# Half of an MLP's down projection by seven half-size products in five chunks of eight

## The chip, the cores and the metric

One NeuronCore of one Trainium2 chip runs the whole program. The metric is the device time in microseconds of one execution; the figure before is the median of three runs. One more execution was taken with the profiler, and all rows quoted here come from it.

## The reference, cut to what matters

Two layers over 512 tokens of width 1024. Each layer ends with a squared-ReLU MLP of hidden width 4096, added to the scaled residual and normalised:

```python
def sq_relu_mlp(h, w_up, w_down):
    return jnp.square(jax.nn.relu(h @ w_up)) @ w_down

for layer in range(DEPTH):          # DEPTH = 2
    mix = mixer_a(...) if layer < N_A else mixer_b(...)
    h = layer_norm(DN_ALPHA * h + mix, ln_g[layer, 0], ln_b[layer, 0])
    h = layer_norm(DN_ALPHA * h + sq_relu_mlp(h, mlp_w_up[layer], mlp_w_down[layer]),
                   ln_g[layer, 1], ln_b[layer, 1])
```

Everything is float32. The kernel splits each operand of a large product into a high part `hi` (rounded to the matmul's fp32r format) and a low part `lo = x - hi`, and adds three matmuls: hi by hi, hi by lo, lo by hi.

## The kernel before, in words

**The MLP's chunks.** `mlp` cuts the hidden width into eight chunks (`c`) of 512 features. A pass of the chunk loop does two halves (`n` = 0, 1). A half has an *up phase*, which makes 256 features of the **next** chunk's hidden tile (a `Pair` of feature blocks), and then a *down phase*, which multiplies the present chunk's hidden tile by the columns `n*512` to `n*512+511` of the down weights and adds the result to `res`.

**The up phase.** A `Pair` does its 1024 x 256 by 512 product by a Winograd form of Strassen's scheme: seven products `m1`, `m6`, `m2`, `m7`, `m5`, `m4`, `m3`, in this order, each of 12 matmuls with 256 moving columns. Its weight sums `sa` and `sb` are four instructions on GpSimd (lines 1058 to 1061), each of 128x512. `split0`, `split_b`, `split_a` and `split2` make the hi parts on ScalarE (a cast, line 975) and the lo parts on VectorE (a subtraction, line 976). VectorE reads the partial sums out of PSUM in between: `u2` (line 1107) after `m6`, `u3` (line 1117) after `m7`, and the `r` pieces (lines 1122, 1126, 1130). As `m6`, `m7` and `m4` accumulate in one PSUM tile, `m7` waits for `u2`'s read, `m4` for `u3`'s, and `m3` for the first `r` read.

**The down phase.** For each of four token tiles, `down` issues 12 matmuls of 512 moving columns (4 contraction blocks times three), and VectorE adds the PSUM tile to `res` (line 1149). The weights come as two slabs of 128x1024 (`dn_slab`, `wload`: a DMA at line 105, a cast at line 108 on ScalarE, a subtraction at line 109 on VectorE).

**Between the phases.** While the down phase runs, the weights of the next pair arrive (line 1056), GpSimd makes its four sums, and `split0`, `split_b`, `split_a` prepare it. `close` squares the hidden pieces and splits them (`hh` on ScalarE, `hl` on VectorE, line 983).

**What sets the order.** Each engine runs its instructions in a fixed order. A planner sets it when the program is built, from the order of the source and the readiness that it expects; `behind(a, b)` forces `a` behind `b` on one engine. Raw weights pass through four slots of 4 KB per partition (tag `wr`), hi and lo parts through five each (`wh`, `wl`). All the weight DMAs are issued by SyncE's queue, in order. The small `pad` tiles shift the addresses of the tiles behind them. Chunk 7's down projection is `downs_last`, with the layer norm between its tiles.

Of the kernel before, what the change touches and what calls it, by code (L numbers as in the profile page):

```python
# [11 lines left out]
F32 = mybir.dt.float32  # L12
# [38 lines left out]
def trunk(ctx: ExitStack, tc: tile.TileContext, xT, xn, memT, wk, wq, wv, wqm, wz, wmk, wmv, wo0, wo1, up, dn,  # L51
# [31 lines left out]
    def nm(s):  # L83
        uid[0] += 1
        return f"{s}_{uid[0]}"
# [3 lines left out]

    def mmt(n="mm"):  # L90
        return pmm.tile([P, 512], F32, tag="mm", name=nm(n))

# [3 lines left out]
    def fr(ap):  # L96
        return ap.bitcast(F32)
# [762 lines left out]

    def load_gb(i):
        g_t = late[0].tile([P, D], F32, tag="lng", name=nm("lng"), bufs=1)
        b_t = late[0].tile([P, D], F32, tag="lnb", name=nm("lnb"), bufs=1)
# [61 lines left out]
    lnp = late[0]  # L925
    gb0 = load_gb(0)
    cosT = lnp.tile([P, NT, 32], F32, tag="cosT", name="cosT")
# [32 lines left out]

    def mlp(pool, layer, last, gb0):
        NC = 8
# [4 lines left out]
        def f4(shape, n):  # L967
            return pool.tile(shape, F32, tag="f4", name=nm(n), bufs=5)

# [16 lines left out]
        def new_hid():  # L986
            return hid_tiles(F32R)
# [23 lines left out]
        def ups_second(hid):  # L1011

            for f in range(2):
                w = wload(up[layer, 4 + f], [P, KT, P])
                ps = mmt("up")
                feature_major(ps, w, x_all(XH), x_all(XL))
                r = f4([P, 512], "relu")
# [8 lines left out]
        def x_sums():  # L1026
# [3 lines left out]
            if layer == 0:  # L1030
                f11, f12, f21, f22 = (xf[j][:, :, t] for j in range(2) for t in (tA, tB))
            else:
                f11, f12, f21, f22 = t1, *(f4([P, 4, HT], n) for n in ("f12", "f21", "f22"))
                for f, x in ((f11, x11), (f12, x12), (f22, x22), (f21, x21)):
                    V.tensor_tensor(f, fr(x[0]), fr(x[1]), op=ALU.add)
# [17 lines left out]
        def up_load(f, e):  # L1053
            raw = [wpool[0].tile([P, KT, P], F32, tag="wr", name=nm("wr"), bufs=wpool[1]) for _ in range(2)]
            for i in range(2):
                SY.dma_start(raw[i], up[layer, f + i])
            sa, sb = (f4([P, 2, 4, P], n) for n in ("sa", "sb"))
            e.tensor_tensor(sa[:, 0], raw[1][:, kA], raw[1][:, kB], op=ALU.add)  # L1058
            e.tensor_tensor(sb[:, 0], sa[:, 0], raw[0][:, kA], op=ALU.subtract)  # L1059
            e.tensor_tensor(sa[:, 1], raw[0][:, kA], raw[1][:, kA], op=ALU.subtract)  # L1060
            e.tensor_tensor(sb[:, 1], raw[0][:, kB], sb[:, 0], op=ALU.subtract)
            return raw, sa, sb

# [8 lines left out]
        class Pair:  # L1072


            def __init__(self, f0, e=G):
                self.f0 = f0
                self.raw, self.sa, self.sb = up_load(f0, e)

            def split0(self, first):
                hi, lo = split(self.raw[0], [P, KT, P], first=first)  # L1080
                self.A11, self.A12 = (hi[:, kA], lo[:, kA]), (hi[:, kB], lo[:, kB])

            def split_b(self):
                hi, lo = split(self.sb, [P, 2, 4, P])
                self.S2, self.S4 = ((hi[:, i], lo[:, i]) for i in range(2))

            def split_a(self, first=None):
                hi, lo = split(self.sa, [P, 2, 4, P], first=first)
                self.S1, self.S3 = ((hi[:, i], lo[:, i]) for i in range(2))

            def split2(self, first_act=None):
                self.A22 = split(self.raw[1][:, kB], [P, 4, P], "w2h", first_act=first_act)

# [15 lines left out]
            def m2(self):  # L1109
                product(self.a, self.A12, xq["B21"], False, True)  # L1110
                self.r = f4([P, 2, 512], "r")
                A.activation(self.r[:, 0, tA], self.a, AF.Relu)

# [10 lines left out]
            def m4(self):  # L1124
                product(self.b, self.A22, xq["T4"], False, True)
                V.tensor_tensor(self.r[:, 1, tA], self.s1, self.b, op=ALU.add)

# [23 lines left out]
        def dn_slab(c, n, i, *first):  # L1151
            return wload(dn[layer, c, n, i], [P, 2, 512], *first)

        def dn_slabs(c, n):
            return [dn_slab(c, n, i) for i in range(2)]

        def downs_last(hid):
            c = NC - 1
# [25 lines left out]
            ln_out(*late_out)  # L1184

        hid, nxt = ups_first()
        gb1 = done = None
        tables = rotary_tables(pool) if layer == 0 else None
        for c in range(NC - 1):
            later = new_hid()  # L1190
            for n in range(2):
                p, nxt = nxt, None
                f0 = 4 * c + 2 * n + 6
                early = c == n == 0
                if p is None:
                    ups_second(later)
                    slabs = dn_slabs(c, n)
                else:
# [18 lines left out]
                    done = p.last  # L1217
                if layer == 0 and c == 0:
                    ln_gain(gb0, ALPHA, n)
# [6 lines left out]
                if f0 < 4 * NC:  # L1226
                    nxt = Pair(f0)
                down(c, 0, n, hid, slabs)
                if nxt:
                    nxt.split0(p and p.r22)  # L1230
                down(c, 1, n, hid, slabs)
                if nxt:
                    nxt.split_b()
                down(c, 2, n, hid, slabs)
                if nxt:
                    nxt.split_a()
                down(c, 3, n, hid, slabs)
            if c == 1:
                gb1 = load_gb(2 * layer + 1)
            hid = later  # L1240
        downs_last(hid)

    with tc.tile_pool(name="mlp0", bufs=2) as mpl:
        mlp(mpl, 0, False, gb0)
    hid_pool[0].close()


    with tc.tile_pool(name="l1", bufs=2) as lp:
# [166 lines left out]

        gb0 = load_gb(2)
        run_steps(LAYER1_ORDER, {"w": load_slabs, "k": shared_kv, "q": projq, "a": attend, "F": flush, "o": out1,
# [3 lines left out]
    with tc.tile_pool(name="mlp1", bufs=2) as mpl:  # L1421
        mlp(mpl, 1, True, gb0)
    hid_pool[0].close()
# [70 lines left out]
```

## Time and profile before

| what | value |
|---|---|
| median of 3 runs | 1158.35 us (1158.11 to 1158.95) |
| profiled execution, its own time | 1156.52 us |
| its span | 1154.8 us |
| granted TensorE clock, mean | 0.994 |
| busy: TensorE matmul / VectorE / ScalarE / GpSimd | 1135.5 / 820.1 / 560.0 / 240.3 us |
| weights loaded for the two MLPs | 64 DMAs of 512 KB each for `up` and for `dn` |

The span is the profiled part of that execution; its own time is 1.7 us more. "Busy" is the union of an engine's instructions; a weight load (PEld) overlaps the matmuls. Since matmuls are pipelined, a matmul's recorded 276 or 390 ns is longer than its pace, which is read from the chain of work (pieces with a start, a length and a count). A row of a group gives the line, engine, operation, output and inputs with shapes, the count, the busy time and the mean of one in ns, then the idle time before and what ended it. Rows of the timeline give start and duration in us.

### The profile page before, as it was taken

Reading aid. Unit: us, or ns where it says so; the run is one execution under the profiler, and the core shown is the slowest. Engines: PE = TensorE matmul, PEld = TensorE weight load, DVE = VectorE, ACT = ScalarE, POOL = GpSimd, SP = SyncE. Lnnn points to the kernel's source line nnn. Section 1 sums busy time; section 2 is a strip of 40 time slices with the busy share of each in tenths; the row PEclk is TensorE's granted clock in tenths of the full one; section 3 lists DMA queues with packets and bytes.
Section 4 is the critical chain, followed back from the end, with each engine's and each line's share of the span. In section 5 each row is a group of like instructions: output and inputs, shape, how many; then the busy total and the mean of one; then the engine's idle time right before and its main releaser. Section 6 shows DMA issues by size and latency. Waiting matters only on the chain.

```text
span 1154.8 us, 19153 instructions
## 1 busy us (share of the span) xinstructions
PE 1135.5 (98%) x7578; PEld 1006.6 (87%) x7578; DVE 820.1 (71%) x1562; ACT 560.0 (48%) x1015; POOL 240.3 (21%) x172
## 2 busy tenths in 40 slices
PE   9999999999999999999999999999999999999997
PEld 9878789989998898998988887778988998989986
DVE  6667789767887676666665968886976665666657
ACT  6454843465584444454443336652645444444531
POOL 1112120011022242423320100000042432424203
PEclk9999999899999999999999999999999999999999
DMA  8522132304313243322334231102332332323311
GB/s 298 162 75 78 47 94 66 102 19 172 103 56 128 92 130 108 109 93 91 117 103 127 77 108 55 56 20 74 110 128 92 104 116 91 110 93 110 108 56 73
DMA packets 41258, 114.11 MB, mean 99 GB/s; under 512 B 11536, under 2 KB 12304, under 8 KB 41168
## 3 DMA queue, kind: packets, MB, share of 16 engines
q1 hardware_dynamic: 40736, 112.10, 29.9%
q8 instruction: 59, 0.97, 0.3%
q10 hardware_dynamic: 432, 0.79, 0.2%
q14 instruction: 31, 0.25, 0.1%
HBM read 109.46 MB, written 3.41 MB: 98 GB/s over the span
## 4 chain that ended last, share of the span: by engine, by line
PE 87%; DVE 6%; issue 2%; ACT 2%; POOL 1%; DMA 0%; DVEq 0%; ACTq 0%; POOLq 0%; SPq 0%
PE dn L69 30%; PE upb L69 9%; PE upd L69 6%; PE upa L69 6%; PE wo L69 5%; PE up L69 4%; PE kq L69 4%; PE projqMM L69 3%; PE proj_zMM L69 3%; PE v L69 3%; PE ov L69 1%; PE ssc L69 1%; DVE wl L109 1%; PE VM L69 1%; PE spt L72 1%
## 5 line engine op out<-in xcount | busy, mean ns | idle before, releaser
L108 ACT CAST wh<-wr 128x1024 fp32r<-128x1024 f32 (+1 forms) x124 | 130.5, 1053 | 218.8 <-PE dn L69 154.8
L109 DVE TENSOR_TENSOR wl<-wr,wh 128x1024 fp32r<-128x1024 f32 (+1 forms) x124 | 168.4, 1359 | 69.7 <-ACT wh L108 69.3
L69 PE MATMUL dn<-wh,hh 128*128 128x512 f32 (+1 forms) x516 | 200.2, 388 | 0.0
L69 PE MATMUL dn<-wh,hl 128*128 128x512 f32 (+1 forms) x516 | 200.1, 388 | 0.0
L69 PE MATMUL dn<-wl,hh 128*128 128x512 f32 (+1 forms) x516 | 200.1, 388 | 0.0
L1149 DVE TENSOR_TENSOR res<-res,dn 128x512 f32<-128x512 f32 (+1 forms) x121 | 82.1, 678 | 64.4 <-PE dn L69 64.3
L69 PEld LDWEIGHTS dn<-wh,hl 128*128 128x128 f32 x516 | 96.9, 188 | 19.9
L69 PEld LDWEIGHTS dn<-wh,hh 128*128 128x128 f32 x516 | 96.9, 188 | 18.9
L69 PEld LDWEIGHTS dn<-wl,hh 128*128 128x128 f32 x516 | 96.9, 188 | 18.9
L1058 POOL TENSOR_TENSOR sa<-wr 128x512 f32<-128x512 f32 x26 | 37.1, 1427 | 358.3 <-DMA wr<-in_up_dram 358.3
L825 POOL TENSOR_TENSOR rs<-rs,nhalf 128x1 f32<-128x1 f32 x16 | 13.0, 815 | 307.4 <-DVE rs L824 253.6
L69 PE MATMUL upb<-TH,wh 128*128 128x256 f32 x216 | 60.3, 279 | 0.0
L69 PE MATMUL upd<-XL,wh 128*128 128x256 f32 x216 | 59.8, 277 | 0.5 <-DVE XL L1204 0.5
L69 PE MATMUL upd<-XH,wh 128*128 128x256 f32 x216 | 59.8, 277 | 0.2 <-DVE r L1122 0.2
L69 PE MATMUL upa<-XL,wh 128*128 128x256 f32 x216 | 59.9, 277 | 0.0
L69 PE MATMUL upd<-XH,wl 128*128 128x256 f32 x216 | 59.7, 276 | 0.0
L69 PE MATMUL upa<-XH,wl 128*128 128x256 f32 x216 | 59.7, 276 | 0.0
L69 PE MATMUL upb<-TL,wh 128*128 128x256 f32 x216 | 59.7, 276 | 0.0
L69 PE MATMUL upb<-TH,wl 128*128 128x256 f32 x216 | 59.7, 276 | 0.0
L1060 POOL TENSOR_TENSOR sa<-wr,wr 128x512 f32<-128x512 f32 x26 | 59.1, 2272 | 0.0
L1059 POOL TENSOR_TENSOR sb<-sa,wr 128x512 f32<-128x512 f32 x26 | 54.7, 2104 | 0.0
L975 ACT CAST wh<-wr 128x1024 fp32r<-128x1024 f32 x27 | 28.5, 1054 | 53.6 <-PE upa L69 53.6
(414 smaller groups left out, 3253.5 us busy)
## 6 DMA issues: line engine op xcount, KB each, us to landing
wr<-in_up_dram SPq DMA_DIRECT2D x64, 512.0 KB, 3.7
wr<-in_dn_dram SPq DMA_DIRECT2D x64, 512.0 KB, 3.8
wr<-in_wo_dram SPq DMA_DIRECT2D x16, 512.0 KB, 4.1
wr<-in_bw_dram SPq DMA_DIRECT2D x8, 512.0 KB, 4.2
wr<-in_wk_dram SPq DMA_DIRECT2D x6, 512.0 KB, 4.3
wr<-in_wq_dram SPq DMA_DIRECT2D x6, 512.0 KB, 3.5
wr<-in_wv_dram SPq DMA_DIRECT2D x6, 512.0 KB, 3.5
wr<-in_wz_dram SPq DMA_DIRECT2D x4, 520.0 KB, 3.9
```

Source lines behind the costliest of these rows:

```text
L69: return self.note(nc.tensor.matmul(*args, **kw))
L72: return self.note(nc.tensor.transpose(*args, **kw))
L108: behind(A.copy(hi, raw), first_act)
L109: behind(V.tensor_sub(lo, raw, fr(hi)), first)
L825: G.tensor_tensor(rs, rs, nhalf[:, 0:1], op=ALU.pow)
L975: behind(A.copy(hi, raw), first_act)
L1058: e.tensor_tensor(sa[:, 0], raw[1][:, kA], raw[1][:, kB], op=ALU.add)
L1059: e.tensor_tensor(sb[:, 0], sa[:, 0], raw[0][:, kA], op=ALU.subtract)
L1060: e.tensor_tensor(sa[:, 1], raw[0][:, kA], raw[1][:, kA], op=ALU.subtract)
L1149: V.tensor_tensor(dst, dst, ps, op=ALU.add)
```

## The change

In chunks 2 to 6 (`SD`) of both layers, the down projection's columns 512 to 1023 are computed by the seven-product scheme (`Down`: the hidden tile is the left factor, cut by contraction blocks and by token halves; the weights are the right one, cut by contraction blocks and by 256 columns). Columns 0 to 511 stay as plain products, as two `Quarter`s of 256 columns each, one in each half. All the down matmuls of these chunks have 256 moving columns. The sums of the hidden tile (`Sums`, four GpSimd instructions of 128x512) and those of the weights (four more in `Down`) are new, and so are the splits of the sums. Partial results stay in PSUM and are accumulated further while VectorE adds each state to the place of `res` that it belongs to. Down weights are loaded as four tiles of 256 columns (two DMAs of 256 KB each). Splits get forced places behind named reads. Tags for PSUM tiles become one per bank; `f4` goes from five buffers to three with new tags `r` (three) and `tb` (one). The layer norm's gain and shift rows move to other tiles and are loaded at other places, and the reserved scratch of SBUF shrinks.

```diff
+    def mmt(n="mm", bank=None):
+        if bank is None:
+            bank = turn_of[0] % 3
+            turn_of[0] += 1
+        return pmm.tile([P, 512], F32, tag=f"mm{bank}", name=nm(n), bufs=1)
...
-            return pool.tile(shape, F32, tag="f4", name=nm(n), bufs=5)
+            return pool.tile(shape, F32, tag="f4", name=nm(n), bufs=3)
+        def rt(shape, n):
+            return pool.tile(shape, F32, tag="r", name=nm(n), bufs=3)
+        def tb(n):
+            return pool.tile([P, 4, 256], F32, tag="tb", name=nm(n), bufs=1)
...
+        SD = range(2, NC - 1)
+        nA, nB = slice(512, 768), slice(768, 1024)
+        class Quarter:
+            def __init__(self, c, m):
+                self.c, self.m = c, m
+                self.raw = columns(c, 0, m)
+            def split(self, *first):
+                self.w = split(self.raw, [P, 4, 256], "wh", *first)
+            def tile(self, t, hid):
+                (hh, hl), (wh, wl) = hid, self.w
+                ps = smt("dnq")[:, 0:256]
+                for k in range(4):
+                    h, l = (x[:, k, t * P:(t + 1) * P] for x in hid)
+                    T.matmul(ps, h, wh[:, k, :], start=k == 0, stop=False)
+                    T.matmul(ps, h, wl[:, k, :], start=False, stop=False)
+                    T.matmul(ps, l, wh[:, k, :], start=False, stop=k == 3)
+                dst = res[:, t, self.m * 256:self.m * 256 + 256]
+                return V.tensor_tensor(dst, dst, ps, op=ALU.add)
+        def columns(c, n, m):
+            raw = wpool[0].tile([P, 4, 256], F32, tag="wr", name=nm("wr"), bufs=wpool[1])
+            for i in range(2):
+                SY.dma_start(raw[:, 2 * i:2 * i + 2, :], dn[layer, c, n, i][:, :, m * 256:m * 256 + 256])
+            return raw
+        class Down:
+            def __init__(self, c):
+                self.R0, self.R1 = (columns(c, 1, m) for m in range(2))
+                self.tb = tb("tb")
+            def sums(self, first):
+                b11, b21, b12, b22 = (r[:, i:i + 2, :] for r in (self.R0, self.R1) for i in (0, 2))
+                t3 = self.tb[:, 0:2, :]
+                behind(G.tensor_tensor(t3, b22, b12, op=ALU.subtract), first)
+                G.tensor_tensor(b12, b12, b11, op=ALU.subtract)
+            def sums_2(self):
+                t1, b22 = self.R1[:, 0:2, :], self.R1[:, 2:4, :]
+                G.tensor_tensor(self.R0[:, 0:2, :], b22, t1, op=ALU.subtract)
+            def sums_3(self, first):
+                behind(G.tensor_tensor(self.tb[:, 2:4, :], self.R0[:, 2:4, :], self.R0[:, 0:2, :], op=ALU.subtract),
+                       first)
...
+            def product(self, ps, h, f, t, w, start, stop, rows, cols):
+                (hh, hl), (wh, wl) = h, w
+                for j in range(2):
+                    tk = slice(t.start + j * P, t.start + j * P + P)
+                    for k in range(2):
+                        a, b = (x[:, f + k, tk] for x in h)
+                        T.matmul(ps[:, j, :], a, wh[:, k, :], start=start and j == 0 and k == 0, stop=False,
+                                 skip_group_check=True)
+                        T.matmul(ps[:, j, :], a, wl[:, k, :], start=False, stop=False, skip_group_check=True)
+                        T.matmul(ps[:, j, :], b, wh[:, k, :], start=False, stop=stop and k == 1, skip_group_check=True)
+                for rw, cl in zip(rows, cols):
+                    dst = res[:, rw.start // P:rw.stop // P, cl]
+                    self.out = V.tensor_tensor(dst, dst, ps, op=ALU.add)
...
+        class Sums:
+            def __init__(self, r0, r1):
+                self.r = r0, r1
+                a11, a21, a12, a22 = (r[:, :, t] for r in self.r for t in (tA, tB))
+                G.tensor_tensor(a22, a21, a22, op=ALU.add)
+                G.tensor_tensor(a21, a11, a21, op=ALU.subtract)
+                G.tensor_tensor(a11, a22, a11, op=ALU.subtract)
+                self.last = G.tensor_tensor(a12, a12, a11, op=ALU.subtract)
...
+                if fast and n == 0:
+                    q = Quarter(c, 0)
+                    d = Down(c)
+                    d.hid = hid
+                    d.sums(s_.last)
...
                     p.m6()
-                    p.split2(None if early else done)
-                    slabs = [dn_slab(c, n, 0, p.u2_in, p.m1_out)] if early else dn_slabs(c, n)
+                    p.split2(None if early else done, p.u2_in if fast else None)
+                    if not fast:
+                        slabs = [dn_slab(c, n, 0, p.u2_in, p.m1_out)] if early else dn_slabs(c, n)
+                    elif n == 0:
+                        q.split(p.u2_in, p.m1_out)
+                    else:
+                        d.split_1(p.u2_in, p.m1_out)
                     p.m2()
                     p.m7()
...
+                    if fast and n == 0:
+                        d.split_0(p.u3_in, p.m2_out)
+                        d.sums_2()
+                    if fast and n == 1:
+                        q.split(p.u3_in, p.m2_out)
                     p.m5()
+                    if fast and n == 0:
+                        d.split_t2(p.r22, p.m2_out)
+                        d.s = [s_.split(0, p.r22, p.m2_out)]
+                    if fast and n == 1:
+                        d.s.append(s_.split(1, p.r22, p.m2_out))
                     p.m4()
+                    if fast and n == 1:
+                        d.split_2(p.r21, p.m2_out)
                     p.m3()
...
                 if f0 < 4 * NC:
                     nxt = Pair(f0)
...
+                if n == 1 and c + 1 in SD:
+                    sums = Sums(rs_[0], rs_[1])
...
+                elif n == 0:
+                    d.sums_3(nxt.sums)
+                    q.tile(0, hid)
+                    d.m1()
+                    nxt.split0(d.out, p.last)
+                    q.tile(1, hid)
+                    d.m2()
+                    nxt.split_b(d.out, p.last)
+                    o = q.tile(2, hid)
+                    d.m6()
+                    nxt.split_a(o, p.last)
+                    q.tile(3, hid)
+                    q = Quarter(c, 1)
+                else:
+                    d.m5()
+                    if nxt:
+                        nxt.split0(d.out, p.last)
+                    q.tile(0, hid)
+                    d.m7()
+                    o = q.tile(1, hid)
+                    if nxt:
+                        nxt.split_b(o, p.last)
+                    d.m3()
+                    if nxt:
+                        nxt.split_a(d.out, p.last)
+                    q.tile(2, hid)
+                    q.tile(3, hid)
+                    d.m4()
-            if c == 1:
-                gb1 = load_gb(2 * layer + 1)
+            s_ = sums
+            if c == NC - 2:
+                gb1 = load_gb(2 * layer + 1, *(f4([P, D], n) for n in ("lng", "lnb")))
             hid = later
...
-    nc = bacc.Bacc("TRN2", target_bir_lowering=False, num_devices=1)
+    nc = bacc.Bacc("TRN2", target_bir_lowering=False, num_devices=1, dynamic_dma_scratch_size=256)
```

More of the change, by code (lines that the diff above doesn't have):

```diff
@@ L959, in rotary_tables, with mlp @@
         yield
-    def mlp(pool, layer, last, gb0):
+    def mlp(pool, layer, last):
         NC = 8
@@ new lines, in mlp, with split @@
+        class Sums:
[6 more added lines that the diff above has]
+                self.last = G.tensor_tensor(a12, a12, a11, op=ALU.subtract)
+            def split(self, i, first, first_act):
+                hi, lo = (pool.tile([P, 2, 512], F32R, tag=f"S{n}{i}", name=nm(f"S{n}{i}"), bufs=1) for n in "HL")
+                behind(A.copy(hi, self.r[i]), first_act)
+                behind(V.tensor_sub(lo, self.r[i], fr(hi)), first)
+                return hi, lo
@@ L1184, in downs_last @@
             ln_out(*late_out)
+        pool.tile([P, 16], F32, tag="pad5", name=nm("pad5"), bufs=1)
+        gbt = [pool.tile([P, 2, 512], F32, tag=f"S{n}0", name=nm("gb"), bufs=1).rearrange("p a b -> p (a b)")
+               for n in "HL"]
+        for n in "HL":
+            pool.tile([P, 2, 512], F32, tag=f"S{n}1", name=nm("gb"), bufs=1)
+        pool.tile([P, 48], F32, tag="pad6", name=nm("pad6"), bufs=1)
+        if layer == 0:
+            gb0 = load_gb(0, *gbt)
         hid, nxt = ups_first()
@@ L1188, in mlp @@
         tables = rotary_tables(pool) if layer == 0 else None
+        sums = None
+        rs_ = {}
         for c in range(NC - 1):
             later = new_hid()
+            fast = c in SD
             for n in range(2):
```

97 lines of the change are left out of this document (62 added, 35 removed).

## The prediction

> **What bounds the kernel now.** I read the page first (busy shares, the chain that ended last), then the chain through one half of a chunk, then the busy times of one chunk.
>
> ```profile
> PE 1135.5 (98%) x7578; PEld 1006.6 (87%) x7578; DVE 820.1 (71%) x1562; ACT 560.0 (48%) x1015; POOL 240.3 (21%) x172
> ...
> PE 87%; DVE 6%; issue 2%; ACT 2%; POOL 1%; DMA 0%; DVEq 0%; ACTq 0%; POOLq 0%; SPq 0%
> ...
> 423.23 1.38 PE upa L69 x12
> 424.60 1.36 PE upb L69 x12
> 425.96 1.36 PE upa L69 x12
> ...
> 431.40 1.36 PE upd L69 x12
> 432.76 10.89 PE dn L69 x48
> ...
> 930.10:971.07 40.97, 40.97 (x266) 37.19 (x265) 25.69 (x33) 18.58 (x23) 14.24 (x8) 1.00 0.32 103
> ...
> 654.81 5.65 PE ropeMM L69 x48
> ```
>
> The chain lies 87% on TensorE. A half of a chunk is seven up products (one of 1.38, six of 1.36, so 9.54 us) and 48 down matmuls (10.89 us), with no gap: 20.43 us, or 40.87 us per chunk. In the chunk at 930 us VectorE was busy for 25.7 of 41 us, ScalarE for 18.6 and GpSimd for 14.2. So TensorE bounds the MLPs, at the full granted clock (1.00), and a down matmul saved is time saved as long as no other resource fills up.
>
> **TensorE, per changed chunk.** Removed: 96 matmuls of 512 columns at 10.89/48 = 226.9 ns, 21.78 us. Added: 96 of 256 columns for the quarters and 7 x 12 = 84 for the products, 180 in all. A 256-column matmul takes 1.36/12 = 113.3 ns in the up products, which share the MLP's slots with the new ones, and 5.65/48 = 117.7 ns in `ropeMM`, whose stationary side is token slices as in the new ones. By the first, 20.40 us; by the second, 21.19. I take the first: today's down matmuls pace at twice 113.4 with the same hidden tiles. Saved: 1.38 us (0.59 at least), which makes a chunk 39.49 us (40.28) if TensorE still bounds it. Ten chunks change (five in each layer).
>
> The Trainium skill (TensorE: Matmul & The Clock Gate, Back-to-back issue gap) gives the gap of a warm matmul as N/2.4 plus 2.5 ns, so two halves cost more than a whole. By that formula the saving would be 1.06 us per chunk; the rows here show 113.3 against 226.9 ns, no surcharge, and I keep them.
>
> **What the other engines get.**
>
> ```profile
> L1149 DVE TENSOR_TENSOR res<-res,dn 128x512 f32<-128x512 f32 x8 | 5.5, 682 | 4.8 <-PE dn L69 4.8
> ...
> L1117 DVE TENSOR_TENSOR u<-m,upb 128x256 f32<-128x256 f32 x2 | 0.8, 422 | 3.5 <-PE upb L69 3.5
> ...
> L108 ACT CAST wh<-wr 128x1024 fp32r<-128x1024 f32 x4 | 4.2, 1054 | 10.9 <-PE dn L69 10.9
> ...
> 413.06 1.22 DVE L976 TENSOR_TENSOR wl<-wr,wh 128x1024 fp32r<-128x1024 f32 x1
> 414.19 1.22 DVE L976 TENSOR_TENSOR wl<-sb,wh 128x1024 fp32r<-128x1024 f32 x1
> ...
> 478.94 0.68 DVE L976 TENSOR_TENSOR w2l<-wr,w2h 128x512 fp32r<-128x512 f32 x1
> 479.54 0.68 DVE L1149 TENSOR_TENSOR res<-res,dn 128x512 f32<-128x512 f32 x1
> ```
>
> ScalarE: four slab casts become seven of 128x1024 and a half one (two quarters, `R0`, `R1`, `tb`, two of `Sums`; `T2`): 3.5 x 1.05 = 3.7 us more, 18.6 + 3.7 = 22.3 of 39.5 us. Hidden by the matmuls.
>
> VectorE: the same 3.5 subtractions more at a pitch of 1.13 us (413.06 to 414.19), and eight adds of 682 ns become eight of 256 columns (422) and seven of 512: 25.7 + 4.0 + 2.7 = 32.4 of 39.5 us, if nothing makes it wait.
>
> GpSimd: eight sums per chunk become sixteen.
>
> **The shared path.** This is where I expect the gain to go. Four sums and two slab subtractions in today's chunk:
>
> ```profile
> 483.38 1.31 POOL L1058 TENSOR_TENSOR sa<-wr 128x512 f32<-128x512 f32 x1 [13.43 <-DMA wr<-in_up_dram]
> 484.65 2.30 POOL L1060 TENSOR_TENSOR sa<-wr,wr 128x512 f32<-128x512 f32 x1
> 486.91 2.27 POOL L1059 TENSOR_TENSOR sb<-sa,wr 128x512 f32<-128x512 f32 x1
> 489.26 1.31 POOL L1061 TENSOR_TENSOR sb<-wr,sb 128x512 f32<-128x512 f32 x1
> ...
> 484.29 1.48 DVE L109 TENSOR_TENSOR wl<-wr,wh 128x1024 fp32r<-128x1024 f32 x1 [1.76 <-ACT wh L108]
> 485.70 0.68 DVE L1149 TENSOR_TENSOR res<-res,dn 128x512 f32<-128x512 f32 x1
> 486.30 1.74 DVE L109 TENSOR_TENSOR wl<-wr,wh 128x1024 fp32r<-128x1024 f32 x1
> 487.96 0.41 DVE L1107 TENSOR_TENSOR u<-m,upb 128x256 f32<-128x256 f32 x1
> ```
>
> Alone a sum takes 1.31 us and a subtraction 1.22. Together they take turns: the subtraction issued at 486.30 ends at 488.04, 1.09 us after the sum before it ended (486.95); the sum issued at 486.91 ends at 489.18, 1.14 us after that subtraction. Adds that read PSUM are not delayed (0.68 at 485.70). So GpSimd's sums and VectorE's instructions with two SBUF inputs must fit one after the other into a chunk.
>
> The Trainium skill (SBUF — State Buffer, SBUF: two separate sides) says the same in stronger words: the pair of ports that the two engines share is an exclusive lock held for a whole instruction, against a VectorE operation with two SBUF inputs or in a two-port mode. By that rule the holds add up, as they do here; if the ports shared their bandwidth instead, there would be no such sum and the chunk would be TensorE's 39.49 us, the first rival.
>
> Holds in a changed chunk: VectorE has 15 subtractions of 1.13 (six for pairs, two `hl`, two quarters, `R0`, `R1`, `tb`, two sums) and three half ones of 0.60 (two `w2l`, `T2`; 478.94 to 479.54): 18.75 us. GpSimd has 16 sums of 1.14 (queued) to 1.31 (alone); I take 1.20, since most will be queued: 19.2. Together 37.95 us of 39.49, 96%; today it is 12 x 1.13 + 2 x 0.60 + 8 x 1.20 = 24.4 of 40.87, 60%.
>
> That leaves 1.5 us of idle path, and one hole is longer.
>
> ```profile
> wr<-in_up_dram SPq DMA_DIRECT2D x64, 512.0 KB, 3.7
> wr<-in_dn_dram SPq DMA_DIRECT2D x64, 512.0 KB, 3.8
> ...
> GB/s 234 266 8 0 16 0 52 242 214 0 0 0 60 301 171 250 226 8 0 0 270 234 4 16 0 0 75 309 123 0 0 0 32 298 179 218 270 20 0 0
> ...
> 472.77 0.33 SPq L1056 DMA_DIRECT2D wr<-in_up_dram  x1
> ...
> lng<-in_lng_dram SPq DMA_DIRECT2D x4, 512.0 KB, 4.1
> ```
>
> By four slots in turn, the second half's pair takes the slot of `R1`, which `split_1` frees: `m6` ends 2.74 us into the half, `u2` 0.33 later, `w2l` 0.60, the subtraction 1.13, so at 4.8; SyncE's issue takes 0.33, landing 3.7, and the second 512 KB some 1.75 more at the 300 GB/s that the row's best slices show. GpSimd can start at 10.6. It should have ended the first half's pair sums so that `split_b` (1.05 cast, 1.13 subtraction) is ready for `m6` at 1.38, and does `sums_3` behind them: it falls idle at about 0.4. In these 10.2 us VectorE holds the path for `split_b`, `split_a`, `w2l`, `R1`, the quarter, `s[1]` and `tb`, 6 x 1.13 + 0.60 = 7.4. Idle: 2.8 us.
>
> Elsewhere the queues meet badly. In the first half's up phase GpSimd still has the sums of the hidden tile and of `Down`, so every subtraction can wait 1.20 for the path, and behind it in VectorE's queue stand `u2`, `u3` and the first `r` read, each due within one product (1.36 us) or TensorE stops. The worst is 1.20 + 1.13 + 0.33 - 1.36 = 1.3 us each, 3.9 in all; the least is 0. With half of them met, at half the price, 1.0: an estimate.
>
> Chunk: 37.95 + 2.8 + 1.0 = 41.75 us, 0.88 above today's 40.87 (ends: 39.49, if the idle is overlapped, and 43.5, with sums at 1.31). Ten chunks: +8.8.
>
> **Edits together at nothing.** The tags, slots and scratch: no DMA here is written by GpSimd. The same down bytes come in eight DMAs of 256 KB instead of four of 512, 4 x 0.33 us more of SyncE's issue; rows of 1 KB may land later than 3.8 us, at worst twice that, 7.6. Cover: a quarter is issued behind `sums_3`, about 9 us before its first tile; with 7.6 and 2.2 for its split it would be 1 us late. Gain and shift rows (4.1 us each) now load in chunk 6, whose second half fetches no pair; they delay four slabs whose first use is 10 us later. None of this lies on the chain: 0, ends -1 and +2.
>
> **The sum.** The profiled execution's own time is 1156.52 us, 1154.8 span and 1.7 around it; with +8.8 it is 1165.3. The median shown lies 1.83 above that execution, so 1167.1.
>
> **The rivals.**
> *The path has room and TensorE stays the bound* (the other side). It decides where holds and idle come below 40.87: with 3.8 us idle, at (40.87 - 18.75 - 3.8)/16 = 1.145 us per sum, and the row above shows 1.14 for one queued sum, so it is near. For it: the forced places put each subtraction right behind a read, which spares the reads, and the sums may be issued earlier than four slots in turn allow. Against: 96%. Down to 39.49 it gives 1158.35 - 13.8 = 1144.5; at 117.7 ns 1152.5. Chance 0.36.
> *The two cancel*: 40.87 again, 1158.35. Chance 0.10.
> *GpSimd's chain is late as well.* In one period `split_1`, the load, four pair sums, four of `Sums`, `sums`, `sums_2`, four pair sums, `split_b` and `m6` follow each other: fifteen sums at 1.31, and the eleven or so subtractions that get in between, make 43.5 us or more; late quarters add to it. +26, 1184. Chance 0.12.
> The forecast has 0.42.
>
> **How the numbers follow.** Under 0.2% (2.3 us) a measurement of this kernel can hardly tell from no change. Faster 0.36, same 0.10, slower 0.42 + 0.12 = 0.54. The predicted time is the forecast's 1167. Its own range is 1161 to 1176; as the first rival holds more than 0.2, the range goes down to 1146, leaving out its best end, and up to 1178, leaving out most of the third.
>
> **What would show it.** Right: a changed chunk of 41 to 43 us; GpSimd's sums and VectorE's two-input subtractions at 1.6 to 2.4 us; TensorE's gaps in front of `m7`, `m4` or `m3` ended by VectorE, or in front of `m6` by a split; 113 ns between new matmuls. Wrong: chunks of 39.5 to 40.3 us without gaps; sums waiting for DMAs in a part of the period in which I have them queued; or a pace of new matmuls over 118 ns, which the rows don't show.

## The result and the profile after

The changed kernel takes 1179.37 us (median of four runs, 1178.30 to 1182.67) beside 1158.65 us for the kernel before on the same chip: ratio 1.0176, 95% interval 1.0159 to 1.0193. That is 20.7 us slower. The forecast was 1167.0, with a range up to 1178; the sign was right, the size was not. The profiled execution is the slowest of the four, 1182.67 us with a span of 1180.9.

The page of the changed kernel: engines, the chain that ended last, the down weights' transfers.

```profile
PE 1148.5 (97%) x8418; PEld 1050.5 (89%) x8418; DVE 935.4 (79%) x1672; ACT 586.0 (50%) x1055; POOL 369.7 (31%) x252
...
PE 74%; DVE 13%; issue 5%; ACT 4%; POOL 2%; DMA 1%; SPq 0%; DVEq 0%; POOLq 0%; ACTq 0%
...
wr<-in_dn_dram SPq DMA_DIRECT2D x80, 256.0 KB, 3.6
```

TensorE has 840 more instructions and is busier (1148.5 after 1135.5 us), although the products were to take work away. The chain has gone from 87% to 74% TensorE, and from 6% to 13% VectorE. Transfers with 1-KB rows land in 3.6 us (median): that bound of the prediction falls away.

The chain through a changed chunk of layer 1 (start, duration, what):

```profile
1025.85 1.42 PE upa L69 x12
1027.27 1.43 PE upb L69 x12
...
1028.91 0.21 issue
1029.13 1.34 DVE w2l L986
1030.47 1.14 DVE wl L986
1031.61 1.02 issue
1032.63 0.42 DVE u L1127
...
1037.63 1.44 PE dns L69 x12
1039.07 1.44 PE dnq L69 x12
...
1049.19 1.36 PE upa L69 x12
```

Two things are seen. Twelve new matmuls take 1.44 us, so 120 ns each and not 113.3; the up products behind them run at 1.42 (118 ns) until a wait lets them fall back to 1.36. And the chain leaves TensorE for a `w2l` of 1.34 us (0.68 alone) and a `wl`, with `u` (L1127) late behind them.

One chunk of layer 1, from its first up product to the next chunk's (length, then busy us and instructions of TensorE, weight load, VectorE, ScalarE, GpSimd; granted clock, DMA share, GB/s), before:

```profile
1002.24:1043.11 40.87, 40.87 (x266) 37.10 (x265) 25.47 (x33) 18.59 (x22) 14.22 (x9) 1.00 0.32 104
```

and after:

```profile
1025.69:1067.56 41.87, 41.70 (x351) 41.30 (x350) 36.25 (x44) 21.50 (x26) 26.89 (x17) 1.00 0.31 102
```

Where the 20.7 us lie: the ten changed chunks, from the first up product of chunk two to the end of chunk six, are 10.6 us longer in the two profiles (6.9 in layer 0, 3.7 in layer 1). About half of the loss lies outside the changed chunks.

### The profile page after: what moved, and what is told of

It is laid out like the page before. It is cut to its first block, busy times and chain, and to the rows that moved or that the text cites. A ratio compares the mean times of both kernels' runs of the same rounds, so it can differ in the third digit from the quotient of the medians.

```text
span 1180.9 us, 21127 instructions
## 1 busy us (share of the span) xinstructions
PE 1148.5 (97%) x8418; PEld 1050.5 (89%) x8418; DVE 935.4 (79%) x1672; ACT 586.0 (50%) x1055; POOL 369.7 (31%) x252
## 4 chain that ended last, share of the span: by engine, by line
PE 74%; DVE 13%; issue 5%; ACT 4%; POOL 2%; DMA 1%; SPq 0%; DVEq 0%; POOLq 0%; ACTq 0%
PE dn L69 10%; PE dnq L69 8%; PE upb L69 8%; PE dns L69 7%; PE wo L69 5%; PE upd L69 5%; PE upa L69 4%; PE kq L69 4%; PE projqMM L69 3%; PE proj_zMM L69 3%; PE v L69 3%; PE up L69 2%; DVE wl L986 2%; DVE wl L115 2%; PE ov L69 1%
## 5 line engine op out<-in xcount | busy, mean ns | idle before, releaser
L986 DVE TENSOR_TENSOR wl<-wr,wh 128x1024 fp32r<-128x1024 f32 x67 | 100.4, 1498 | 0.0
L69 PE MATMUL dnq<-wh,hl 128*128 128x256 f32 x320 | 90.5, 283 | 0.0
L69 PE MATMUL dnq<-wh,hh 128*128 128x256 f32 x320 | 90.5, 283 | 0.0
L69 PE MATMUL dnq<-wl,hh 128*128 128x256 f32 x320 | 90.4, 283 | 0.0
L69 PE MATMUL dn<-wh,hh 128*128 128x512 f32 (+1 forms) x196 | 75.9, 387 | 2.0 <-DVE res L1157 1.3
L69 PE MATMUL dn<-wh,hl 128*128 128x512 f32 (+1 forms) x196 | 75.6, 386 | 0.0
L69 PE MATMUL dn<-wl,hh 128*128 128x512 f32 (+1 forms) x196 | 75.5, 385 | 0.0
L69 PEld LDWEIGHTS dnq<-wh,hl 128*128 128x128 f32 x320 | 61.3, 192 | 0.0
L69 PEld LDWEIGHTS dnq<-wl,hh 128*128 128x128 f32 x320 | 61.3, 192 | 0.0
L69 PEld LDWEIGHTS dnq<-wh,hh 128*128 128x128 f32 x320 | 61.3, 192 | 0.0
```

What stands on the lines that cost most here:

```text
L69: return self.note(nc.tensor.matmul(*args, **kw))
L986: behind(V.tensor_sub(lo, raw, fr(hi)), first)
```

## The experiments

Three theories. **P**: TensorE's pace in the changed chunks. **S**: the path that GpSimd and VectorE share. **E**: the edits around the chunks, which the prediction took together at nothing. All ratios are to the kernel before on the same chip.

**No changed chunk, all other edits kept.**

```
-        SD = range(2, NC - 1)
+        SD = range(0)
```

> The changed kernel with no changed chunk: all down projections are plain 512-column tiles as before; kept are the new tags and buffer counts, the smaller DMA scratch, the gain and shift rows in MLP tiles and their later loads. Theory E (the edits outside the chunks cost time): of the 26 us between the two profiled executions some 15 lie outside chunks two to six, so this kernel stays 8 to 15 us above the kernel before, 1166 to 1173 us. Theory P (TensorE's pace in the changed chunks) and theory S (the path that GpSimd and VectorE share) put the whole loss into the chunks: 1158 to 1161 us, no change.

Measured: 1165.39 us, ratio 1.0046 (1.0033 to 1.0060), +5.3 us. Theory E holds, with less than its lower bound of 8 us: a part of the 15 us that two single profiles showed was not the edits'. The rows that show a cause are SyncE's and VectorE's at the start of layer 1; this kernel:

```profile
664.30 0.33 SPq L1456 DMA_DIRECT2D pm<-kv  x1
```

```profile
660.35 1.17 DVE L115 TENSOR_TENSOR wl<-wr,wh 128x1024 fp32r<-128x1024 f32 x1
...
662.82 1.41 DVE L893 SCALAR_TENSOR_TENSOR res<-res,rs,lnb 128x512 f32<-128x512 f32 x2
```

and the kernel before:

```profile
652.41 0.33 SPq L1254 DMA_DIRECT2D pm<-kv  x1
```

Layer 1's first transfer, `pm`, goes out 0.07 us after the last layer norm has read the shift row `lnb` (662.82 + 1.41). The rows now lie in tiles of the MLP's pool, and layer 1's pool takes the MLP pool's memory over. If its tiles wait for the last reader of that memory (theory E1), the rows put elsewhere should free them. Weight subtractions (`wl`, the row at 660.35) are meanwhile placed ahead of the last layer norm.

**The rows elsewhere.** The same kernel, its last gain and shift rows in the hidden tile's buffer that chunk six has freed:

```
-                gb1 = load_gb(2 * layer + 1, *(f4([P, D], n) for n in ("lng", "lnb")))
+                rows = hid_tiles(F32)[0].rearrange("p k n -> p (k n)")
+                gb1 = load_gb(2 * layer + 1, rows[:, 0:D], rows[:, D:2 * D])
```

> The kernel without changed chunks, with one edit put another way: the last gain and shift rows of each MLP are not in two tiles of the MLP's pool but in the hidden tile's buffer that chunk six has freed. Theory E1 (the rows in the MLP's pool keep that memory until the last layer norm has read them, and layer 1's first tiles, which lie there, wait for it): the 5.4 us are gone, 1158 to 1161 us. Theory E2 (the loss comes from the smaller scratch, the fewer buffers or the rows' place in SyncE's queue): it stays at 1163 to 1167 us.

Measured: 1161.03 us, 1.0016 (1.0007 to 1.0025).

```profile
625.67 0.33 SPq L1457 DMA_DIRECT2D pm<-kv  x1
```

`pm` goes out 39 us earlier, and 3.5 of the 5.3 us are gone. So E1 holds for the larger part, though it had put all of the loss there; what the other 1.8 us are (fewer buffers, the smaller scratch, other places in the queues) was not taken apart.

**The new sums left out.** The eight new sums per chunk on GpSimd (`Down.sums`, `sums_2`, `sums_3`, `Sums`) are gone; `tb` is filled once, everything else stays.

> The changed kernel without the eight new sums per chunk on GpSimd (four of the hidden tile, four of the weights); the splits read the unsummed tiles, so matmuls, casts, subtractions, adds and transfers stay as they are. Theory S (GpSimd's sums and VectorE's two-input subtractions do not fit one after the other): holds fall from some 38 to 28 us per chunk, TensorE becomes the bound at 39.5 to 40.3 us, ten chunks 15 to 23 us shorter: 1156 to 1164 us. Theory P (the new 256-column matmuls take 120 ns and the up products behind them 117.7): a chunk stays near 180 x 0.120 + 168 x 0.1177 = 41.4 us, only the waits go, 0.4 to 1.0 us per chunk: 1170 to 1175 us. Theory E has no part in it.

Measured: 1171.49 us, 1.0090 (1.0072 to 1.0107), 10 us better than the changed kernel. The same chunk:

```profile
1016.49:1057.86 41.37, 41.37 (x350) 41.37 (x349) 32.76 (x44) 21.39 (x26) 12.28 (x8) 1.00 0.32 103
```

TensorE is busy all of it, and 41.37 is 180 x 0.120 + 168 x 0.1177: with every wait gone, a changed chunk is still longer than the 40.87 of before. The time is in P's range and out of S's: S had reckoned with a TensorE of 39.5 to 40.3 us. But the sums cost 10 us too, so which of the two sets the chunk was not settled by this.

**Where the 120 ns come from.** The kernel before had them already, in its last token tile, whose last 512 columns of the down projection are done in two parts of 256:

```profile
1144.52 0.28 PE L69 MATMUL dn<-wl,hh 128*128 128x256 f32 x1
1144.64 0.28 PE L69 MATMUL dn<-wh,hl 128*128 128x256 f32 x1
1144.76 0.28 PE L69 MATMUL dn<-wh,hh 128*128 128x256 f32 x1
```

The starts are 120 ns apart. In the program's memory both operands, `hh` and `wh`, begin 96 bytes past a multiple of 128 (224 past a multiple of 256), while the up products pair `wh` at 96 (224) with `XH` and `TH` at 32 (160). To try the place, the kernel before got its down tiles of chunks two to six in two parts of 256 columns, with the hidden tiles 32 floats longer and shifted by a chunk's own offset (the splitting in two is not shown):

```
-        return [hid_pool[1].tile([P, 4, 512], dt, tag=n, name=nm(n)) for n in ("hh", "hl")]
+        ts = [hid_pool[1].tile([P, 2048 + 32], dt, tag=n, name=nm(n)) for n in ("hh", "hl")]
+        return [t[:, off:off + 2048].rearrange("p (k n) -> p k n", k=4) for t in ts]
...
+            return hid_tiles(F32R, 8 * ((c - 2) % 4) if 2 <= c < 7 else 0)
```

> The kernel before, with the down tiles of chunks two to six computed as two parts of 256 columns (192 matmuls of 256 columns instead of 96 of 512, the same adds, no sums, no new slots), and the hidden tiles (the stationary side) laid 0, 32, 64, 96 and 0 bytes further in SBUF in chunks 2, 3, 4, 5, 6. Theory P1 (a 256-column matmul with this kernel's down operands paces at 120 ns because both operands lie at the same place modulo 128 bytes, as wh and hh do): 120 ns in chunks 2 and 6, and 113 to 118 ns in at least one of chunks 3, 4, 5. Theory P2 (it is the width alone, or the order hh-wh, hh-wl, hl-wh): 120 ns in all five, chunks of 42.1 to 42.8 us. Theory S, which takes TensorE's pace as that of the up products: 113.4 ns in all five, chunks of 40.9 us.

Measured, one run: 1192.67 us. The 96 down matmuls of a half chunk, from the first to the next up product (columns as above, of the down instructions alone, without ScalarE and GpSimd); chunks 2, 3, 4, 5 of layer 0 and then of layer 1, so 0, 32, 64, 96 bytes twice:

```profile
457.53:468.93 11.40, 11.40 (x96) 11.35 (x96) 2.06 (x3) 1.00 0.28 92
480.33:491.69 11.36, 11.36 (x96) 11.31 (x96) 2.06 (x3) 1.00 0.30 94
524.68:535.56 10.88, 10.88 (x96) 10.85 (x96) 2.06 (x3) 1.00 0.31 98
567.51:578.90 11.39, 11.39 (x96) 11.35 (x96) 2.06 (x3) 1.00 0.28 92
971.00:982.50 11.50, 11.50 (x96) 11.45 (x96) 2.06 (x3) 1.00 0.27 93
993.77:1005.29 11.52, 11.52 (x96) 11.47 (x96) 2.06 (x3) 1.00 0.28 91
1039.10:1050.40 11.30, 11.30 (x96) 11.26 (x96) 2.07 (x3) 1.00 0.29 95
1083.32:1094.52 11.20, 11.20 (x96) 11.15 (x96) 2.06 (x3) 1.00 0.28 95
```

Divided by 96: 118.8, 118.3, 113.3, 118.6 ns in layer 0 and 119.8, 120.0, 117.7, 116.7 in layer 1. So it is not the width alone (theory P2, 120 ns everywhere), nor are these matmuls as fast as the up products (theory S, 113.4 everywhere).

The same offset is not the same place in the two layers. Chunks use the two buffers of the hidden tiles in turn, the layers begin with different ones, and the 32 added floats put the buffers 128 bytes apart modulo 256: `hh` begins at 96 in one and at 224 in the other, where the kernel before has 224 in both. The eight rows are thus eight places: 96, 0, 160, 64 bytes past a multiple of 256 in layer 0, and 224, 128, 32, 192 in layer 1. Only at 160, against `wh` at 224, does the pace reach 113.3; these are the two places of the up products. The place modulo 128 (theory P1) is not the rule: at 0 and 128 the operands lie differently by it, and the pace is 118.3 and 120.0. At 224 it is 119.8, close to the 120 of the kernel before, which lies there too.

**Whole tiles at the same offsets.** As above, with the 512-column products of the kernel before.

> The kernel before, its down tiles whole (512 columns), with the hidden tiles laid 0, 32, 64, 96 and 0 bytes further in chunks 2 to 6. If the place matters to the switch from one matmul to the next, a 512-column matmul pays the same few ns: 226.9 at 0 bytes (where the 256-column one paid most, 6.6 ns), between 226 and 233 elsewhere. If it is a matter of columns read, twice the 256-column figures: 240, 235, 227 ns.

Measured, one run: 1173.62 us. Half chunks in layer 0: of chunk one, unshifted, then of chunks two, three and four with 0, 32 and 64 bytes.

```profile
415.52:426.42 10.90, 10.90 (x48) 8.83 (x48) 2.05 (x3) 1.00 0.44 147
456.64:467.79 11.15, 11.15 (x48) 8.86 (x48) 2.06 (x3) 1.00 0.28 96
499.49:510.69 11.20, 11.20 (x48) 8.83 (x48) 2.05 (x3) 1.00 0.29 95
540.81:551.80 10.99, 10.99 (x48) 8.83 (x48) 2.05 (x3) 1.00 0.30 97
```

Per matmul 227.1, 232.3, 233.3 and 229.0 ns. Twice the 256-column figures of these places would be 240, 238, 237 and 227, so the few ns are not paid per column; but neither does an instruction pay the same at either width: at 224 bytes 256 columns took 119.8 ns, and 512 take 227.1, the least of the four. Chunks one and two have the same offset and differ by 5 ns, which neither expectation had. They lie in different buffers, at 224 and at 96 bytes modulo 256, and this repeats: in both layers of this run the unshifted half chunks at 224 take 227 ns and those at 96 take 232. So it is the place modulo 256, not 128, that these runs go by; why one place is faster than another is not known.

**The stationary side 64 bytes further in the changed kernel**: hidden tiles of chunks two to six as above with 16 floats, and `pad5`, `pad6` changed from 16 and 48 to 32 floats each, which moves the tiles of `Sums`.

> The changed kernel with the stationary tiles of the changed chunks (hidden tiles of chunks two to six, and the tiles of their sums) laid 64 bytes further in SBUF; nothing else. Theory P1 (120 ns comes from both operands lying at the same place modulo 128 bytes): the new matmuls pace at 113.4 ns, 20.4 instead of 21.6 us per chunk, and the up products at 113.4 to 117.7; a chunk of TensorE's is 39.5 to 40.2 us, with 0.5 us of waits 40.0 to 40.7; ten chunks 11 to 18 us below the changed kernel: 1161 to 1168 us. Theory S (the shared path allows no less than some 41.5 us per chunk, whatever TensorE does): the gain turns into waits for GpSimd's sums and VectorE; within 4 us of the changed kernel, 1175 to 1180 us.

Measured: 1176.82 us, 1.0147 (1.0132 to 1.0163), 3.4 us better.

```profile
1019.24:1061.06 41.82, 41.45 (x350) 40.91 (x349) 36.69 (x44) 21.51 (x26) 28.99 (x17) 1.00 0.32 102
```

**The same without the new sums.**

> The run before it without the eight new sums per chunk on GpSimd (the splits read the unsummed tiles). It gives the chunk that TensorE alone would allow at the better pace. Theory P1: 39.5 to 40.2 us per chunk without waits, 1151 to 1158 us with the 5.4 us outside the chunks that the kernel without changed chunks showed. The distance to the run before it is the price of the sums at this pace: under 0.5 us per chunk by P1, over 1 us per chunk by theory S.

Measured: 1166.51 us, 1.0059 (1.0045 to 1.0073).

```profile
1012.76:1053.76 41.00, 41.00 (x350) 41.00 (x349) 32.60 (x45) 21.50 (x26) 14.06 (x8) 1.00 0.32 104
```

Its neighbours are 40.6 us: TensorE gained 0.4 to 0.8 us per chunk, less than the 1.2 to 1.9 that P1 gave, as part of the matmuls stayed at 117.7 ns. Here too the chunks differ by buffer: those whose hidden tiles lie at 160 bytes modulo 256 fall to 113.3 in a part of their down products, and those at 32, the one shown among them, stay at about 117.8. With the sums the chunk is 41.82, as before the shift, and the sums now cost 10.2 us in all. S holds: TensorE's gain turns into waits.

**Both edits together**, shift and rows.

> The changed kernel with both edits: stationary tiles 64 bytes further, last gain and shift rows in the freed hidden tile. If P1 and E1 hold they add up: 5 us below the run with the shift alone, 1155 to 1163 us, about the kernel before or a little faster. If theory S holds it stays above 1169 us.

Measured: 1173.58 us, 1.0124 (1.0107 to 1.0141): 2.7 us better than the shift alone, where E1 had said 5; far from 1155 to 1163, and above 1169, as S said.

**The moving side 64 bytes further instead.** The changed chunks' weights lie 16 floats into slots of 1056 floats, the hidden tiles stay, the rows are in the freed hidden tile, and the rotary scratch lies in the tables' own tiles:

```
+        t = wpool[0].tile([P, 1024 + 32], F32R, tag=n, name=nm(n), bufs=5)[:, off:off + 1024]
...
-        ang, rn = (pool.tile([P, NT, 32], F32, tag=n, name=n, bufs=1) for n in ("ang", "rn"))
+        ang, rn = cosT, sinT
```

> The changed kernel with the down weights of the changed chunks (the moving side of their matmuls) laid 64 bytes further inside their slots, all but the half-size one; the hidden tiles stay. Then the new matmuls and the up products have the same places modulo 128 bytes for stationary (96) and moving side (32). The rotary scratch lies in the tables' own tiles to make room, and the last gain and shift rows in the freed hidden tile. Theory P3 (the shift of the stationary side left 117.7 ns in both kinds because places swapped roles at every turn between up and down): 113 to 115 ns throughout, TensorE's chunk 39.5 to 39.9 us. What is then left is theory S's: with the sums in the way the chunk stays at 41.3 to 41.8 us, 1170 to 1175 us; without a bound by the path (theory P) 40.0 to 40.4 us, 1157 to 1161 us. If P3 is wrong the pace stays at 117 to 118.

Measured: 1176.44 us, 1.0148 (1.0132 to 1.0163). Its chain and its chunk:

```profile
1047.58 1.36 PE upb L69 x12
...
1051.70 1.41 PE dnq L69 x12
```

```profile
1019.58:1061.42 41.84, 41.20 (x351) 40.73 (x350) 36.50 (x44) 21.51 (x26) 27.08 (x17) 1.00 0.31 102
```

P3 was wrong for the new matmuls, which stay at 117.7 ns, and right for the up products, which run at 113.3. The plain tiles of the other chunks went from 227 to 231 ns: their places modulo 128 are what they were, but slots of 1056 floats lie 128 bytes apart modulo 256 in turn. And the chunk is 41.84 once more, a little over the 41.3 to 41.8 of theory S.

**The same without the new sums.**

> The run before it without the eight new sums per chunk on GpSimd (the splits read the unsummed tiles). P3: chunks of 39.5 to 39.9 us, 1150 to 1155 us. If P3 is wrong, 40.6 to 41.1 us as with the stationary side shifted. The distance to the run before it prices the sums: some 2 us per chunk by theory S with P3, 0.5 by theory P.

Measured: 1159.67 us, 0.9997 (0.9987 to 1.0008).

```profile
1008.00:1048.27 40.27, 40.27 (x350) 40.27 (x349) 32.31 (x44) 21.50 (x26) 13.19 (x8) 1.00 0.33 105
```

TensorE alone needs 40.27 us here (between the two forecasts, 39.5 to 39.9 and 40.6 to 41.1), 40.6 to 41.0 with the stationary side shifted, and 41.37 in the changed kernel; with the sums the three chunks take 41.82 to 41.87. In this kernel the sums cost 1.6 us per chunk of layer 1 and 17 us in all.

**Path or chain?** The sums could cost so much because they and VectorE's subtractions take turns (S), or because GpSimd's own row of sums, loads and slots is too long (C, the prediction's third rival). So this kernel keeps all sixteen sums, and takes eight of VectorE's eighteen subtractions off the path: their low parts are copies of the raw tile by ScalarE (here, and likewise in `Sums`).

```
             behind(A.copy(hi, raw), first_act)
+            if shape[-1] == 256:
+                behind(A.copy(lo, raw), first_act)
+            else:
-            behind(V.tensor_sub(lo, raw, fr(hi)), first)
+                behind(V.tensor_sub(lo, raw, fr(hi)), first)
```

> The kernel with the down weights laid 64 bytes further and all sixteen sums, whose low parts in the changed chunks (two quarters, R0, R1, tb, the half-size one, two hidden sums) are copies of the raw tile by ScalarE and no longer subtractions with two SBUF inputs on VectorE: some 8.5 us per chunk less on the shared path, while GpSimd keeps all its sums and their order. Theory S (GpSimd and VectorE take turns on the path): the same relief as by leaving eight sums out, which took 17 us off: chunk 40.3 to 40.9 us, 1160 to 1167 us. Theory C (it is GpSimd's own chain of sixteen sums, loads and slots that sets the chunk, whatever VectorE does): chunk 41.6 to 41.9 us, 1172 to 1177 us.

Measured: 1159.00 us, 0.9999 (0.9987 to 1.0011).

```profile
1006.64:1046.91 40.27, 40.27 (x350) 40.27 (x349) 25.91 (x35) 28.65 (x34) 24.24 (x17) 1.00 0.33 106
```

All sums are there (GpSimd has 17 instructions, 24.2 us), and the chunk is TensorE's 40.27, as without the new sums. So GpSimd's row alone is not what sets the chunk: theory C is out. VectorE's row alone is not it either, as the kernel without new sums keeps all of VectorE's instructions. That the two meet on the path, and not in a subtraction that waits for a late sum to end, is seen in the kernel with all sums and all subtractions: in two chunks of layer 1 VectorE never stands idle for GpSimd, but its `w2l` take 1.38 us on average instead of 0.69 without the new sums, and those of `Sums` 1.74 instead of 1.22.

**Half of the new sums**: the four of the hidden tile are left out, those of the weights stay.

> The same kernel, subtractions on VectorE, with only the four new sums of the hidden tile left out per chunk (its splits read the unsummed tiles) and the four of the weights kept. All eight cost some 17 us. Theory S: each sum on the path costs alike, half of them gives back half, 8 us: 1166 to 1170 us. Theory C puts the price into the weights' chain (load, sums, sums_2, sums_3, split): under 4 us back, 1172 to 1176 us.

Measured: 1161.46 us, 1.0025 (1.0016 to 1.0035).

```profile
1006.52:1046.89 40.37, 40.37 (x350) 40.36 (x349) 33.95 (x44) 21.51 (x26) 18.61 (x12) 1.00 0.32 105
```

Half of the sums gives back 14 of 17 us: neither S (half) nor C (under 4 us) had that form. By the prediction's prices, an estimate, the holds are 18.75 + 12 x 1.20 = 33.2 of 40.3 us (82%) with twelve sums, and next to nothing is lost in layer 1; with sixteen they are 94% of the same chunk, and it grows by 1.6 us. This looks like a limit that is met near its end, not like a price per sum; only this half of the sums was tried.

No kernel here beats the one before: with pace and rows mended and half of the sums or the subtractions taken away, it is no faster than before.

## Why the prediction was wrong, step by step

**Which step failed.** The sum had +8.8 us and the kernel lost 20.7. The one term of the sum, the ten chunks, measured 10.6. What broke it are two terms at nothing: "Edits together at nothing", with ends of -1 and +2, cost 5.3 us, and the unchanged chunks, which no step mentions, lost 4.3. TensorE's saving failed as a mechanism as well, but moved the sum little, since the path sets the chunk: mending a part of the pace gained 3.4 us.

**TensorE's saving: wrong.** The step "I take the first: today's down matmuls pace at twice 113.4 with the same hidden tiles" failed. 180 new matmuls at 120 ns are 21.6 us for the 21.78 removed, and the up products behind them slowed to 117.7 in addition; without sums a chunk is 41.37, 0.50 above before, where 39.49 was forecast. That "the rows don't show" a pace over 118 ns was a row not looked for: the 256-column down matmuls of the last tile stood in the profile of before at 120, at the places modulo 256 where those of 512 columns took 226.9. The formula of the Trainium skill (TensorE: Matmul & The Clock Gate, Back-to-back issue gap) gives 109.2 ns for 256 columns and 215.8 for 512; every row here lies above it (113.3 to 120, 227 to 234). What decides among these paces stays open in part: the place modulo 256 does, and so does something that lasts from one group of matmuls to the next.

**The shared path: right in mechanism, and in the size of the chunk.** Forecast 41.75 us per chunk; measured 41.87 in chunks four to six of layer 1 (41.0 and 41.7 in the two before them), and 41.8 to 41.9 in chunk four whatever TensorE's own floor was. The hole is there too: in chunk four of layer 1 GpSimd waits 10.1 us for the second half's pair, 10.2 by the forecast, though from 2 us earlier on. The parts of the sum (holds, idle, waits of the reads) were not measured singly. VectorE's 36.3 busy us where 32.4 were forecast contain its waits for the path: without the new sums the same instructions take 32.8. That the two engines hold each other up agrees with the rule of the Trainium skill (SBUF — State Buffer, SBUF: two separate sides), which says that their shared ports are an exclusive lock. The first rival ("the path has room") is refuted by the 41.8 us over a floor of 40.27, and the third (GpSimd's chain, 43.5 us per chunk) by the kernel with ScalarE's copies, although its 1184 lay closer to the outcome. ScalarE's 21.5 us are near the 22.3 forecast.

**The ten chunks: 10.6 for 8.8.** Layer 1 gave 3.7, less than its half of 8.8, and layer 0 gave 6.9. There chunks two to six start at 428.8, 470.9, 514.6, 557.4 and 599.1 us; the second of them takes 43.7. Chunks two to four lost 5.4 us in layer 0 and 1.9 in layer 1; five and six lost 1.5 and 1.8. The sum had left out that chunks two to four of layer 0 also hold the rotary tables. The chain in chunk four:

```profile
522.80 0.41 DVE r L1132
523.21 2.19 DVE SL L1290
525.39 1.72 DVE w2l L986
527.12 0.33 DVE r L1136
527.45 0.94 DVE rn L955
528.41 1.28 DVE ang L956
```

A subtraction for `Sums` (1.22 alone) takes 2.19, a half one (0.68 alone) 1.72, and behind them stand the rotary instructions, two of which hold the chain for 2.2 us. That the tables are there was readable in the code; no run moved them.

**The unchanged chunks: 4.3 us that no step had.** In chunks zero and one, three up phases of layer 0 and two of layer 1 take 10.4 to 10.5 us instead of 9.5 to 9.8. One of the five, the changed kernel's GpSimd and then VectorE:

```profile
407.33 1.31 POOL L1068 TENSOR_TENSOR sa<-wr 128x512 f32<-128x512 f32 x1 [15.81 <-DMA wr<-in_up_dram]
```

```profile
407.35 2.37 DVE L115 TENSOR_TENSOR wl<-wr,wh 128x1024 fp32r<-128x1024 f32 x1 [1.76 <-ACT wh L114]
...
411.91 0.41 DVE L1117 TENSOR_TENSOR u<-m,upb 128x256 f32<-128x256 f32 x1
```

The kernel without changed chunks at the same point:

```profile
404.33 2.15 POOL L1068 TENSOR_TENSOR sa<-wr 128x512 f32<-128x512 f32 x1 [14.47 <-DMA wr<-in_up_dram]
```

```profile
404.08 1.23 DVE L115 TENSOR_TENSOR wl<-wr,wh 128x1024 fp32r<-128x1024 f32 x1 [1.76 <-ACT wh L114]
```

Whoever comes first has the path. In the changed kernel the sum is 0.02 us ahead of the slab's subtraction, which then takes 2.37 us, and `u` and TensorE wait; in the other the subtraction is 0.25 us ahead and the sum waits, which costs nothing. Why the sum comes earlier was not tried, and the cause stays open. It is not the new sums: without them the five phases still take 10.0 to 10.4 us, and in the two single runs, which have no new sums either, three and two of them take 10.1 to 10.5.

**The edits taken together at nothing: +5.3.** The transfers were indeed free (3.6 us). The rows were looked at as load on SyncE's queue, and that was not their price: 3.5 of the 5.3 us came from the memory that they kept from layer 1; the other 1.8 stay open. No step asked who takes over a tile's memory and when its last reader is done.

By place, 10.6 + 4.3 us from the two profiles and 5.3 by the ratio make 20.2 of the 20.7. From the ratios alone: the new sums 10.0 (changed kernel against no new sums), all else that comes with the changed chunks 5.1 (no new sums against no changed chunk), the edits around them 5.3. The 5.1 are not the pace alone: by the profiles of these two kernels 3.4 of them lie in the five late up phases.

## What to carry to other kernels

Before a pace is borrowed from a like instruction, look for the very instruction, with its shape and its operands, elsewhere in the profile: here two partial tiles at the end had it. Add up, over one period, what GpSimd's sums and VectorE's instructions with two SBUF inputs hold of their common path; by estimated holds next to nothing was lost here at 82%, 1.6 us per chunk at 94%, and a faster TensorE did not shorten that chunk. When a tile moves to another pool, find its last reader and what takes its memory next.

## What was not expected of the hardware

A waiting GpSimd sum got no turn between VectorE's instructions where these came without a gap. At the start of layer 1's MLP of the changed kernel, GpSimd and VectorE:

```profile
853.99 9.40 POOL L1068 TENSOR_TENSOR sa<-wr 128x512 f32<-128x512 f32 x1 [15.32 <-DVE TL L156]
863.36 1.31 POOL L1070 TENSOR_TENSOR sa<-wr,wr 128x512 f32<-128x512 f32 x1
```

```profile
853.72 1.22 DVE L1049 TENSOR_TENSOR f<-f,f 128x1024 f32<-128x1024 f32 x1
...
861.54 0.69 DVE L986 TENSOR_TENSOR w2l<-wr,w2h 128x512 fp32r<-128x512 f32 x1
```

A sum of 1.31 us took 9.40, until ten VectorE instructions with two SBUF inputs, issued back to back from 853.72, had ended at 862.23. In the chunks, where VectorE stops for ScalarE's casts and for PSUM, the rows show the two taking turns.

And a matmul of the same shape on the same kind of operands paces at 113.3 to 120 ns (227 to 234 with 512 columns) by where the tiles lie modulo 256 bytes and by what ran before: a shift of 64 bytes was worth up to 0.5 us on 96 matmuls.
